# A hybrid block and two diffusion-transformer layers in float32 on one Trainium2 core: head-norm factors on 128 partitions, single-stream weights 64 bytes on, and four smaller edits

## The chip, the cores and the metric

One NeuronCore of a Trainium2 chip runs the whole program; seven cores are idle. The metric is the device time of one execution in microseconds (us). The kernel before was run three times: 2473.56, 2482.21 and 2483.57 us, median 2482.21.

## The reference, cut to what matters

All inputs and results are float32. A first block (attention in three dilations, a state-space scan, a gated feed-forward network) acts on 256 tokens `x` of width 1024. A second block of two layers acts on `x` and on 256 context tokens `xc`, each layer with its own modulation vectors.

```python
def first_block(x, ...):
    h = x + hybrid_mixer(rmsnorm(x, norm1_w), w_in, conv_w, ...)   # q,k,v,z,xbc,dt,gates = xn @ w_in
    h = h + swiglu(rmsnorm(h, norm2_w), w_ffn_in, w_ffn_out)       # D_FF = 2816
    return rmsnorm(h, final_norm_w)

def second_block(x, c, ctx, ...):
    xc = ctx
    for l in range(2):
        mx, mc = split(silu(c) @ w_mod[l] + b_mod[l], 9), split(silu(c_ctx) @ w_mod[l] + b_mod[l], 9)
        x  = x  + 0.5 * mx[2] * swiglu_2(modulate(rms_norm(x),  mx[0], mx[1]), *ffn1)
        xc = xc + 0.5 * mc[2] * swiglu_2(modulate(rms_norm(xc), mc[0], mc[1]), *ffn1)
        h, hc = modulate(rms_norm(x), mx[3], mx[4]), modulate(rms_norm(xc), mc[3], mc[4])
        if l == 0: y, y_c = mix_window_diff(h, hc, ab_w_in, ab_w_out, ...)          # windowed + differential attention
        else:      y, _   = mix_mla_neighbourhood(h, hc, cd_w_in, cd_w_out, ...)    # latent + neighbourhood attention
        x = x + mx[5] * y
        x = x + 0.5 * mx[8] * swiglu_2(modulate(rms_norm(x), mx[6], mx[7]), *ffn2)
        if l == 0: xc = ...  # the same with mc, y_c
    return x

def head_norm(t, gain):              # on every head of q and k in both mixers
    return t * rsqrt(mean(t * t, over the head's 64, 96 or 32 channels) + 1e-6) * gain
```

The causal convolution of the first block has 4 taps and a bias per channel (`conv_w`, `conv_b`). The neighbourhood attention adds a bias of 8 heads that depends on the row and column distance of query and key (`rpb`).

## The kernel before, in words

**Products.** Activations lie with channels on partitions and tokens along the free dimension. Every weight matrix is streamed once, 128 x 1024 floats (512 KB) at a time: SP issues the load (`load_raw`, L113, five buffers `wraw`), ACT rounds a copy to the short float format (`wh`, L120), DVE forms the remainder `wl = raw - wh` (L121); `wh` and `wl` have five buffers each in the pool `wsplit`. The activations are split in the same way (`ah`, `al`; hidden activations `hh`, `hl`). A product of one 128-channel block is three matmuls on PE, `mm3_k`: `wh` by `ah` (L139), `wh` by `al` (L140), `wl` by `ah` (L141), and eight (or six) such blocks add up in one PSUM tile `pm`. The weight tile is the stationary operand and the activation the moving one; in `v_units` (L1165 to L1167), which makes values with tokens on partitions, it is the other way round.

**Streams and units.** `run` goes through a list of units (one stationary tile, one PSUM tile) and of steps woven between them. In the second block, two streams "c" (context) and "x" go side by side: their activations interleave in the tiles `comb`, so that one matmul has 512 columns. The first three units of a run (`head`) and its last ones (`edge`, up to three tiles) are done for each stream alone, with 256 columns. Where a list runs for one stream (the first block, queries, the last network), all matmuls have 256 columns.

**Addresses.** Pools are laid one behind the other in each partition's memory, and unused tiles (`gap`) shift what follows. A weight tile of 1024 floats begins 64 bytes past a multiple of 128; so do the tiles `comb` (also for one stream of them) and the hidden activations of the two-stream networks. The activations of the first block's mixer, its hidden activations and the tile of the last single-stream network begin at a multiple of 128. The split queries `hq`, `lq` begin 96 past a multiple of 128. In what follows "phase" is an address's remainder by 128 bytes.

**Head norms** (`HeadNorm`, in both mixers). Per product block the squares of the heads are summed by a matmul (L1047), the factors `rs` are computed for all blocks of a group, transposed (L1056) and split into one ring tile `rh` of 48 rows: high parts on rows 0 to n-1, low parts on rows 32 to 32+n-1, zeros between. `finish` then spreads a head's factor over its channels with a matmul whose stationary operand is the constant `sel` (48 rows, ones where a factor belongs), L1071, and DVE multiplies by it. These steps are deferred by `later` and so land between the matmuls of other units.

**First block's start.** SP loads `cols` (all small per-channel constants). On DVE, `start` halves the convolution weights, `cw = 0.5 * cols[...]` (L908). The squares of `x` are summed by DVE into `acc` (L322), PE sums them over channels (L345), DVE and ACT take the root, PE spreads the factor (L353) and the first product can start. On POOL's queue the constants and the first block's attention bias (`brow`) are moved.

**Neighbourhood bias.** `bias_rows` copies the 8 heads' rows 64 times into a scratch tensor in DRAM with 8 transfers of POOL's queue (L1643), DRAM to DRAM. In `mix_cd`, `load_bias` fetches for each head four 64 x 256 pieces from it (L1614, SP's queue) and POOL adds a mask (L1615); four buffers `bias`. `scores_d` asks for the bias two heads ahead and DVE adds it to the scores (L1623). The scores' softmax tiles `e` are a ring of eight in each mixer.

**Differential attention** (`attend_b` in `mix_ab`): scores (L1339, `qbx` 512 columns), softmax, transposes (L1140), values (L1355) and, after four heads, `normed`: a norm over the head's 128 channels with a square tile `ybs` of its own.

**Order.** The scheduler orders every engine's list by the order of the program and by which buffers come free; `mod_tasks` gives 72 pieces per layer of the modulation product (a load `wraw<-w_mod` and one or two DVE operations, L1001) that are woven into the networks.

Of the kernel before, what the change touches and what calls it, by code (L numbers as in the profile page):

```python
# [8 lines left out]
F32 = mybir.dt.float32  # L9
F32R = mybir.dt.float32r  # L10
AF = mybir.ActivationFunctionType
ALU = mybir.AluOpType
# [4 lines left out]
T = 256  # L17
# [51 lines left out]
class Builder:  # L69
    def __init__(self, ctx, tc, A):  # L70
        self.tc, self.nc, self.A, self.ctx = tc, tc.nc, A, ctx
        nc = self.nc
# [3 lines left out]

        self.gap(self.pool(ctx, "gap", 1), 320)
        self.tp = self.pool(ctx, "tmp", 10)
# [36 lines left out]

    def split_w(self, raw, f):
        nc = self.nc
        h = self.w_p.tile([128, 1024], F32R, name="wh")
        lo = self.w_p.tile([128, 1024], F32R, name="wl")
        nc.scalar.copy(h[:, :f], raw[:, :f])  # L120
        nc.vector.tensor_tensor(lo[:, :f], raw[:, :f], h[:, :f].bitcast(F32), op=ALU.subtract)  # L121
        return h, lo
# [79 lines left out]
    def run(self, items, streams, done=None, ko=0, ahead=2):  # L202
# [7 lines left out]
        def prepare(i):  # L210
            if i >= len(units) or i in ready:
                return
            u = units[i]
            f = u.src.shape[2]
            ready[i] = [self.split_w(self.load_raw(u.src[j]), f) for j in range(u.at, u.at + u.n)]

# [247 lines left out]
def block1(K, start_mod):  # L464
# [442 lines left out]
    def start():  # L907
        nc.vector.tensor_scalar(cw, K.cols[:, at:at + 120], 0.5, None, op0=ALU.mult)  # L908

# [178 lines left out]
def head_selectors(K, pool, width, rows, n):  # L1088

    nc, A = K.nc, K.A  # L1090
    at, n2 = COLS[f"sum{width}"]
    sums = K.cols[:rows, at:at + n2]
    raw = K.raw_p.tile([128, 1024], F32, name="wraw")
    sel = pool.tile([48, n * 128], F32R, name=f"sel{width}")
    nc.scalar.dma_start(raw[:48, :n * 128], A[f"sel{width}"])
    nc.vector.tensor_copy(sel, raw[:48, :n * 128])
    return sums, sel


def stacked(K, pool):  # L1100

    zero = K.t1("zero")
    K.nc.vector.memset(zero, 0.0)
    ring = []
    for i in range(4):
        ring.append(pool.tile([48, T], F32R, name=f"rh{i}"))
        K.nc.scalar.copy(ring[i], zero[:48])
    return ring
# [72 lines left out]
def mix_ab(K, streams):  # L1181
# [192 lines left out]
    def normed(po):  # L1374
        yb = sp.tile([128, 4, 128], F32, name="yb", bufs=2)
        nc.scalar.copy(yb, po.rearrange("p (h e) -> p h e", h=4))
        sq = sp.tile([128, 4, 128], F32, name="ybs", bufs=1)
        ss = sp.tile([128, 4], F32, name="yss", bufs=2)
# [32 lines left out]
def mix_cd(K, streams):  # L1411
# [195 lines left out]
    def load_bias(hd):  # L1607
        bias = biases[hd] = sp.tile([128, 2, T], F32, name="bias", bufs=4)
        for t in range(2):
# [28 lines left out]

def bias_rows(K):

    K.rpb = K.dram.tile([64, 8, 7 * 127], F32, name="rpb")
    rows = K.A["rpb"][:, 4:11].rearrange("h r c -> h (r c)").unsqueeze(0).to_broadcast([8, 8, 7 * 127])
    return [lambda i=i: K.nc.gpsimd.dma_start(K.rpb[8 * i:8 * i + 8], rows) for i in range(8)]  # L1643


def block2(K, layers=(0, 1)):
    nc, A = K.nc, K.A
    for layer in layers:
        both = ["c", "x"]

        def norms(i, layer=layer):
            return lambda s: K.norm_stream(s, K.mod(layer, s, i + 1), K.mod(layer, s, i))

        steps = K.pieces(40)
        if layer == 0:
            steps[10:10] = bias_rows(K)
        fctx = ExitStack()
        hid_p = K.pool(fctx, "h1", 14)
        K.ffn(A[f"f1g{layer}"], A[f"f1u{layer}"], [A[f"f1d{layer}{i}"] for i in range(3)], both,
# [96 lines left out]
def constants():  # L1756
# [25 lines left out]
    for name, rows, n in (("sel64", [64, 64], 5), ("sel96", [64, 32], 4)):  # L1782
        sel = np.zeros((48, n, 128), f)
        for b in range(n):
            at = 0
            for e, r in enumerate(rows[:2]):
                sel[[2 * b + e, 32 + 2 * b + e], b, at:at + r] = 1.0
                at += r
        c[name] = sel.reshape(48, n * 128)
    t = np.arange(T)  # L1790
# [131 lines left out]
```

## Time and profile before

| what | value |
|---|---|
| three runs | 2473.56, 2482.21, 2483.57 us (median 2482.21) |
| the profiled execution's own time | 2473.19 us |
| its span, first to last instruction | 2471.4 us |
| mean granted TensorE clock | 0.985 |
| PE busy | 2415.3 us, 98% of the span |
| PEld (weight loads, beside PE) | 2101.6 us, 85% |
| DVE / ACT / POOL busy | 1642.8 / 1064.7 / 34.3 us |
| read from HBM | 359.33 MB, 147 GB/s over the span |

The profiled execution stands 9.0 us under the median of the three runs. Matmuls overlap one another in the trace: one of 256 columns lasts 0.28 us, but the next starts some 0.12 us after it, so rates are read from the distance of the starts, or from the count in a window.

### The profile page before, as it was taken

The numbers are of one execution on the slowest core, as the hardware profiler recorded it, in microseconds if no ns is written. First come the engines' busy times: TensorE is split into PE (matmuls) and PEld (weight loads), VectorE is DVE, ScalarE is ACT, GpSimd is POOL, SyncE is SP. The second block draws the span as 40 slices with busy tenths as digits, with TensorE's granted clock in tenths as the row PEclk, the third lists the DMA queues.
The fourth block names the chain that finished last, engine by engine and source line by source line (L and its number), as shares of the span: only waits on it lengthen the run. The fifth ranks groups of instructions, "written<-read, shape, count | busy, mean of one in ns | idle before, by whom it ended". The sixth has DMA issues, their size and how long they took to land.

```text
span 2471.4 us, 38395 instructions
## 1 busy us (share of the span) xinstructions
PE 2415.3 (98%) x15104; PEld 2101.6 (85%) x15104; DVE 1642.8 (66%) x3016; ACT 1064.7 (43%) x1934; POOL 34.3 (1%) x56
## 2 busy tenths in 40 slices
PE   7999999999999999999999999999999999999999
PEld 6998999999988888886498888888888888876999
DVE  5767787787865666778757666656555555667655
ACT  4566565535632222535743222243222234555443
POOL 3000000000000000000000000000000000000000
PEclk9999899999999999999899999999999999999999
DMA  9455455676454554341014555534555422233554
GB/s 271 153 154 157 134 175 174 212 251 225 148 177 136 170 173 144 112 139 52 1 52 154 165 159 162 165 108 142 180 166 171 150 87 84 100 97 86 169 195 133
DMA packets 113157, 363.38 MB, mean 147 GB/s; under 512 B 21186, under 2 KB 23562, under 8 KB 112976
## 3 DMA queue, kind: packets, MB, share of 16 engines
q1 hardware_dynamic: 109232, 352.58, 45.1%
q0 software_dynamic: 2176, 5.09, 0.9%
q10 hardware_dynamic: 1568, 3.25, 0.4%
q8 instruction: 119, 1.95, 0.3%
q14 instruction: 62, 0.51, 0.1%
HBM read 359.33 MB, written 3.36 MB: 147 GB/s over the span
## 4 chain that ended last, share of the span: by engine, by line
PE 70%; DVE 3%; ACT 2%; issue 1%; DMA 0%; ACTq 0%; DVEq 0%
PE pm L139 20%; PE pm L140 20%; PE pm L141 20%; PE pt L1140 1%; PE pa L1047 1%; PE pm L1339 1%; PE pt L1071 1%; PE pa L1592 1%; DVE wl L121 1%; PE pm L1600 1%; PE pa L1355 1%; PE pm L1279 1%; PE pa L1316 0%; PE pm L1622 0%; PE pm L1165 0%
## 5 line engine op out<-in xcount | busy, mean ns | idle before, releaser
L139 PE MATMUL pm<-ah,wh 128*128 128x256 f32 (+2 forms) x3096 | 1002.9, 326 | 13.1 <-ACT ah L370 10.7
L140 PE MATMUL pm<-al,wh 128*128 128x256 f32 (+2 forms) x3096 | 997.4, 323 | 1.1 <-DVE al L371 1.0
L141 PE MATMUL pm<-ah,wl 128*128 128x256 f32 (+2 forms) x3096 | 996.1, 322 | 0.0
L120 ACT CAST wh<-wraw 128x1024 fp32r<-128x1024 f32 (+4 forms) x535 | 541.0, 1014 | 946.0 <-PE pm L140 750.3
L121 DVE TENSOR_TENSOR wl<-wraw,wh 128x1024 fp32r<-128x1024 f32 (+4 forms) x535 | 627.5, 1176 | 228.3 <-ACT wh L120 225.8
L139 PEld LDWEIGHTS pm<-ah,wh 128*128 128x128 f32 (+1 forms) x3096 | 590.1, 192 | 67.8 <-ACT ah L370 12.3
L140 PEld LDWEIGHTS pm<-al,wh 128*128 128x128 f32 (+1 forms) x3096 | 591.9, 191 | 49.0 <-issue 2.7
L141 PEld LDWEIGHTS pm<-ah,wl 128*128 128x128 f32 (+1 forms) x3096 | 592.2, 191 | 46.6 <-issue 2.3
L140 PE MATMUL pm<-hl,wh 128*128 128x512 f32 (+1 forms) x934 | 312.6, 335 | 0.0
L139 PE MATMUL pm<-hh,wh 128*128 128x512 f32 (+1 forms) x934 | 312.1, 334 | 0.0
L141 PE MATMUL pm<-hh,wl 128*128 128x512 f32 (+1 forms) x934 | 312.1, 334 | 0.0
L1001 DVE SCALAR_TENSOR_TENSOR junk<-wraw,cactc 128x1024 f32<-128x1024 f32 x112 | 137.2, 1225 | 183.1 <-DMA wraw<-w_mod 183.0
L1001 DVE SCALAR_TENSOR_TENSOR junk<-wraw,cactx 128x1024 f32<-128x1024 f32 x144 | 176.1, 1223 | 48.8 <-DMA wraw<-w_mod 46.2
L139 PEld LDWEIGHTS pm<-hh,wh 128*128 128x128 f32 x934 | 175.7, 188 | 18.7
L140 PEld LDWEIGHTS pm<-hl,wh 128*128 128x128 f32 x934 | 175.7, 188 | 18.6
L141 PEld LDWEIGHTS pm<-hh,wl 128*128 128x128 f32 x934 | 175.8, 188 | 18.4
L125 ACT CAST hh<-g 128x512 fp32r<-128x512 f32 (+1 forms) x113 | 59.1, 525 | 228.4 <-DVE g L428 228.4
L428 DVE TENSOR_TENSOR g<-g,pm 128x512 f32<-128x512 f32 (+1 forms) x113 | 64.0, 567 | 55.6 <-PE pm L141 54.1
L126 DVE TENSOR_TENSOR hl<-g,hh 128x512 fp32r<-128x512 f32 (+1 forms) x113 | 63.9, 567 | 0.3
L458 DVE SCALAR_TENSOR_TENSOR xc<-pm,mcol0c,xc 128x256 f32<-128x256 f32 x56 | 26.9, 481 | 53.5 <-PE pm L141 53.3
L424 ACT ACTIVATE g<-pm 128x512 f32<-128x512 f32 (+1 forms) x116 | 55.9, 486 | 2.0 <-PE pm L141 2.0
L1140 PEld LDWEIGHTS pt<-ident,e 128*128 128x128 f32 x272 | 30.7, 145 | 22.0 <-issue 18.6
(425 smaller groups left out, 2260.0 us busy)
## 6 DMA issues: line engine op xcount, KB each, us to landing
wraw<-w_mod SPq DMA_DIRECT2D x144, 512.0 KB, 4.0
wraw<-f1g SPq DMA_DIRECT2D x44, 512.0 KB, 3.9
wraw<-f1u SPq DMA_DIRECT2D x44, 512.0 KB, 4.2
wraw<-f2g SPq DMA_DIRECT2D x44, 512.0 KB, 3.6
wraw<-f2u SPq DMA_DIRECT2D x44, 512.0 KB, 3.6
wraw<-f1d SPq DMA_DIRECT2D x32, 512.0 KB, 3.9
wraw<-f2d SPq DMA_DIRECT2D x32, 512.0 KB, 3.6
wraw<-w_xbc SPq DMA_DIRECT2D x24, 512.0 KB, 3.7
```

Of the source, the lines that this page charges most:

```text
L120: nc.scalar.copy(h[:, :f], raw[:, :f])
L121: nc.vector.tensor_tensor(lo[:, :f], raw[:, :f], h[:, :f].bitcast(F32), op=ALU.subtract)
L125: self.nc.scalar.copy(h, src)
L126: self.nc.vector.tensor_tensor(lo, src, h.bitcast(F32), op=ALU.subtract)
L139: nc.tensor.matmul(out, h[:, c], ah, start=first, stop=False)
L140: nc.tensor.matmul(out, h[:, c], al, start=False, stop=False)
L141: nc.tensor.matmul(out, lo[:, c], ah, start=False, stop=last)
L424: nc.scalar.activation(half(g["g"], s), p, AF.Silu)
L428: nc.vector.tensor_tensor(t, t, p, op=ALU.mult)
L458: self.nc.vector.scalar_tensor_tensor(x, p, gate, x, op0=ALU.mult, op1=ALU.add)
L1001: nc.vector.scalar_tensor_tensor(junk, raw, 1.0, K.cact[s], op0=ALU.mult, op1=ALU.mult, accum_out=K.mcol[layer, s][:, j:j + 1])
L1140: nc.tensor.transpose(p[:, j * 128:(j + 1) * 128], b, K.ident)
```

## The change

1. **Weight tiles.** `split_w` makes tiles of 1088 floats and uses 1024 of them, from float 16 on (64 bytes) where a unit is worked on for one stream alone and its activations come from `comb`, else from float 0. The gap in front of what follows falls from 320 to 64 bytes (the ten tiles grow by 2560 bytes together), so later tiles keep their phase.
2. **Head norms.** `sel` and the ring tiles `rh` have 128 rows; the added rows are zero.
3. **`start`** halves the convolution weights on GpSimd.
4. **`bias_rows`** loads the 8 heads' rows into a tile of 8 partitions and copies them from there, later; it is called once the first network's pool is open.
5. **`normed`** takes its square tile from the ring `e`.
6. **`load_bias`** has three buffers in place of four.

```diff
-        self.gap(self.pool(ctx, "gap", 1), 320)
+        self.gap(self.pool(ctx, "gap", 1), 64)
...
-    def split_w(self, raw, f):
+    def split_w(self, raw, f, at=0):
         nc = self.nc
-        h = self.w_p.tile([128, 1024], F32R, name="wh")
-        lo = self.w_p.tile([128, 1024], F32R, name="wl")
+        h, lo = (self.w_p.tile([128, 1088], F32R, name="w" + n)[:, at:at + 1024] for n in "hl")
...
-            ready[i] = [self.split_w(self.load_raw(u.src[j]), f) for j in range(u.at, u.at + u.n)]
+
+            if two:
+                alone = len(u.streams or streams) == 1 or i < head or i >= n - edge
+            else:
+                alone = self.comb and not self.single and u.lin and u.lin[0] == self.acts
+            ready[i] = [self.split_w(self.load_raw(u.src[j]), f, 16 if alone else 0) for j in range(u.at, u.at + u.n)]
...
     def start():
-        nc.vector.tensor_scalar(cw, K.cols[:, at:at + 120], 0.5, None, op0=ALU.mult)
+        nc.gpsimd.tensor_scalar(cw, K.cols[:, at:at + 120], 0.5, None, op0=ALU.mult)
...
-    sel = pool.tile([48, n * 128], F32R, name=f"sel{width}")
-    nc.scalar.dma_start(raw[:48, :n * 128], A[f"sel{width}"])
-    nc.vector.tensor_copy(sel, raw[:48, :n * 128])
+    sel = pool.tile([128, n * 128], F32R, name=f"sel{width}")
+    nc.scalar.dma_start(raw[:, :n * 128], A[f"sel{width}"])
+    nc.vector.tensor_copy(sel, raw[:, :n * 128])
...
-        ring.append(pool.tile([48, T], F32R, name=f"rh{i}"))
-        K.nc.scalar.copy(ring[i], zero[:48])
+        ring.append(pool.tile([128, T], F32R, name=f"rh{i}"))
+        K.nc.scalar.copy(ring[i], zero)
...
-        sq = sp.tile([128, 4, 128], F32, name="ybs", bufs=1)
+        sq = sp.tile([128, 512], F32, name="e", tag="e", bufs=8).rearrange("p (h e) -> p h e", h=4)
...
-        bias = biases[hd] = sp.tile([128, 2, T], F32, name="bias", bufs=4)
+        bias = biases[hd] = sp.tile([128, 2, T], F32, name="bias", bufs=3)
...
-def bias_rows(K):
+def bias_rows(K, pool):
 
     K.rpb = K.dram.tile([64, 8, 7 * 127], F32, name="rpb")
-    rows = K.A["rpb"][:, 4:11].rearrange("h r c -> h (r c)").unsqueeze(0).to_broadcast([8, 8, 7 * 127])
-    return [lambda i=i: K.nc.gpsimd.dma_start(K.rpb[8 * i:8 * i + 8], rows) for i in range(8)]
+    rows = pool.tile([8, 896], F32, name="rpbrow", bufs=1)[:, :7 * 127]
+    copies = rows.unsqueeze(1).to_broadcast([8, 8, 7 * 127])
+    steps = [lambda: K.nc.gpsimd.dma_start(rows, K.A["rpb"][:, 4:11].rearrange("h r c -> h (r c)"))]
+    return steps + [lambda i=i: K.nc.gpsimd.dma_start(K.rpb[8 * i:8 * i + 8].rearrange("q h u -> h q u"), copies)
+                    for i in range(8)]
...
-        if layer == 0:
-            steps[10:10] = bias_rows(K)
-        fctx = ExitStack()
-        hid_p = K.pool(fctx, "h1", 14)
+        if layer == 0:
+            steps[10:10] = bias_rows(K, hid_p)
...
-        sel = np.zeros((48, n, 128), f)
+        sel = np.zeros((128, n, 128), f)
...
-        c[name] = sel.reshape(48, n * 128)
+        c[name] = sel.reshape(128, n * 128)
```

Three of the edits move instructions. First, POOL's queue from the program's start, before (`mk` are attention masks, `bt` the one-hot table, `rpb` the neighbourhood bias, `brow` and `bias` the first block's own):

```order
L519 DMA mk_136<-mask 128x128
L519 DMA mk_138<-mask 128x128
L1643 DMA rpb<-rpb 64x1x889
L508 DMA brow_108<-ct 8x16x384
L508 DMA brow_109<-ct 8x16x256
```

and with the change:

```order
L523 DMA mk_136<-mask 128x128
L523 DMA mk_138<-mask 128x128
L912 ISA
L912 TENSOR_SCALAR cw<-cols 128x120
L512 DMA brow_108<-ct 8x16x384
L512 DMA brow_109<-ct 8x16x256
```

The halving `cw`, which was the first DVE operation after the memsets (in front of the sums `acc` of L322), stands on POOL between the masks and `brow`; the copy `rpb` has left this place.

Second, SP's queue around the neighbourhood attention (`dmask` is its mask, `f2g` and `f2u` the next network's weights), before:

```order
L113 DMA wraw<-cd_out 128x1024 x8
L1604 DMA dmask<-dmask 128x256
L1614 DMA bias<-rpb 64x4x64 x16
L113 DMA wraw<-f2g 128x1024
L113 DMA wraw<-f2u 128x1024
L1614 DMA bias<-rpb 64x4x64 x16
L113 DMA wraw<-f2g 128x1024
```

and with the change:

```order
L113 DMA wraw<-cd_out 128x1024 x8
L1608 DMA dmask<-dmask 128x256
L1618 DMA bias<-rpb 64x4x64 x12
L113 DMA wraw<-f2g 128x1024
L113 DMA wraw<-f2u 128x1024
L1618 DMA bias<-rpb 64x4x64 x20
L113 DMA wraw<-f2g 128x1024
```

Four bias loads, those of the fourth head, have moved from the first group to the second.

Third, PE's list in the differential attention's second half (`kb`, `qbx` keys and queries, `e` softmax tiles, `pts` their transposes, `yb` the normed outputs), before:

```order
L1339 MATMUL pm<-kb,qbx 128x512
L1355 MATMUL pa<-v,pts 128x128 x2
L1339 MATMUL pm<-kb,qbx 128x512 x5
L1364 MATMUL pt<-ident,yb 128x128 x4
L1140 MATMUL pt<-ident,e 128x128 x2
L1339 MATMUL pm<-kb,qbx 128x512
L1355 MATMUL pa<-v,pts 128x128 x2
L1140 MATMUL pt<-ident,e 128x128 x8
```

and with the change:

```order
L1343 MATMUL pm<-kb,qbx 128x512 x3
L1144 MATMUL pt<-ident,e 128x128 x2
L1343 MATMUL pm<-kb,qbx 128x512
L1144 MATMUL pt<-ident,e 128x128 x2
L1359 MATMUL pa<-v,pts 128x128 x4
L1368 MATMUL pt<-ident,yb 128x128 x4
L1144 MATMUL pt<-ident,e 128x128 x2
L1343 MATMUL pm<-kb,qbx 128x512 x2
```

The run of five score matmuls has broken into smaller groups between transposes.

## Rows read from the trace of the kernel before

**Rows 1.** The page: busy time by engine, and the last chain's shares by engine.

```profile
PE 2415.3 (98%) x15104; PEld 2101.6 (85%) x15104; DVE 1642.8 (66%) x3016; ACT 1064.7 (43%) x1934; POOL 34.3 (1%) x56
...
PE 70%; DVE 3%; ACT 2%; issue 1%; DMA 0%; ACTq 0%; DVEq 0%
```

**Rows 2.** Windows of PE: start:end, us, busy (matmuls), granted clock, DMA share, GB/s.

```profile
484.00:510.00 26.00, 26.00 (x219) 1.00 0.77 257
512.00:532.00 20.00, 20.00 (x178) 1.00 0.69 227
540.00:575.00 35.00, 34.98 (x291) 1.00 0.77 262
2300.00:2335.00 35.00, 35.00 (x311) 1.00 0.67 224
700.00:740.00 40.00, 40.00 (x178) 1.00 0.51 157
```

**Rows 3.** Timeline of PE, latent values: start, us, engine, line, operation, tiles.

```profile
2153.91 0.28 PE L1524 MATMUL pm<-wl,hk 128*128 128x256 f32 x1
...
2154.98 0.28 PE L1524 MATMUL pm<-wl,hk 128*128 128x256 f32 x1
```

**Rows 4.** Windows of all engines (PE, PEld, DVE, ACT, POOL), first block's network.

```profile
540.00:580.00 40.00, 39.98 (x333) 39.69 (x332) 35.44 (x56) 19.99 (x32) 0.00 (x0) 1.00 0.79 267
```

**Rows 5.** Timeline there: DVE's remainder and its first use.

```profile
562.81 1.22 DVE L121 TENSOR_TENSOR wl<-wraw,wh 128x1024 fp32r<-128x1024 f32 x1
...
564.76 0.28 PE L141 MATMUL pm<-ah,wl 128*128 128x256 f32 x1
```

**Rows 6.** Instructions of L1071: count, min/median/max ns, first and last start.

```profile
L1071 PE MATMUL pt<-rh,sel x64: 276/356/384, 1077.4 to 2187.3; 48*128 48x256 f32 x38, 48*64 48x256 f32 x16, 48*96 48x256 f32 x10
```

**Rows 7.** Timeline of PE, values with L1071 between them.

```profile
1135.18 0.38 PE L1071 MATMUL pt<-rh,sel 48*128 48x256 f32 x1
...
1135.74 0.30 PE L1165 MATMUL pa<-wh,ah 128*128 128x320 f32 x1
1135.98 0.38 PE L1071 MATMUL pt<-rh,sel 48*128 48x256 f32 x1
...
1137.34 0.31 PE L1166 MATMUL pa<-wh,al 128*128 128x320 f32 x1
1137.49 0.31 PE L1167 MATMUL pa<-wl,ah 128*128 128x320 f32 x1
```

**Rows 8.** Timeline of the weight loads there.

```profile
1135.60 0.19 PEld L1165 LDWEIGHTS pa<-wh,ah 128*128 128x128 f32 x1
1135.97 0.18 PEld L1071 LDWEIGHTS pt<-rh,sel 48*128 48x128 f32 x1 [0.19 <-issue]
```

**Rows 9.** Timeline of PE: a transposition on 128 rows, and 64-column selectors.

```profile
1098.07 0.60 PE L1056 MATMUL pt<-ident,rs 128*8 128x128 f32 x4
1098.42 0.48 PE L139 MATMUL pm<-ah,wh 128*128 128x512 f32 x1
...
2145.66 0.33 PE L1071 MATMUL pt<-rh,sel 48*64 48x256 f32 x1
...
2146.46 0.33 PE L1071 MATMUL pt<-rh,sel 48*64 48x256 f32 x1
```

**Rows 10.** Timeline of DVE and PE at the start.

```profile
9.19 0.22 DVE L908 TENSOR_SCALAR cw<-cols 128x120 f32<-128x120 f32 x1 [7.78 <-DMA cols<-cols]
...
15.59 1.02 PE L345 MATMUL pt<-ones,acc 128*128 128x1 f32 x4 [3.78 <-DVE acc L322]
```

**Rows 11.** Timeline of SP, DVE and POOL, neighbourhood attention.

```profile
2224.82 12.33 SPq L1614 DMA_DIRECT2D bias<-rpb  x16
...
2229.41 1.27 POOL L1615 TENSOR_TENSOR bias<-bias,dmask 128x512 f32<-128x512 f32 x1 [27.20 <-DMA bias<-rpb]
...
2230.38 0.43 DVE L1623 TENSOR_TENSOR pm<-pm,bias 128x256 f32<-128x256 f32 x1 [0.42 <-PE pm L1622]
```

**Rows 12.** Windows of PE, differential attention (columns as in rows 2).

```profile
1216.00:1230.00 14.00, 13.68 (x38) 0.51 0.00 0
```

More of the change, by code (lines that the diff above doesn't have):

```diff
@@ L1652, in norms @@
             return lambda s: K.norm_stream(s, K.mod(layer, s, i + 1), K.mod(layer, s, i))
+        fctx = ExitStack()
+        hid_p = K.pool(fctx, "h1", 14)
         steps = K.pieces(40)
         if layer == 0:
-            steps[10:10] = bias_rows(K)
-        fctx = ExitStack()
-        hid_p = K.pool(fctx, "h1", 14)
+            steps[10:10] = bias_rows(K, hid_p)
         K.ffn(A[f"f1g{layer}"], A[f"f1u{layer}"], [A[f"f1d{layer}{i}"] for i in range(3)], both,
```

## The prediction

> **What bounds the kernel now.** The page's busy times come first: PE is busy for 98% of the span, and 70% of the last chain runs over it [rows 1]. So time goes only where PE's matmuls follow one another faster, or where PE stood still. The reader should see next that "busy" hides two rates. In the windows [rows 2], all at full clock, 256-column matmuls start every 26.0/219 = 0.1187 us and 35/291 = 0.1203 us where weight tile and activation have the same phase (484 to 510, 540 to 575), but every 20/178 = 0.1124 and 35/311 = 0.1125 us where they are 64 bytes apart (512 to 532, the down products; 2300 to 2335, the last network). The timelines give 0.120 and 0.1133 when no count is cut off at a window's edge; I use 0.0066 us as the difference. Third, the head norms: L1071 is 64 matmuls on 48 rows [rows 6] set between matmuls on 128.
>
> **Weight tiles 64 bytes on.** This changes no instruction, only addresses. From the code, the matmuls whose two operands go from the same phase to 64 apart are 44 x 24 = 1,056 in the first block's network and 1,908 elsewhere: heads of three two-stream networks 432, their tails 324, `ab_qk` 144, `ab_out` 288, `cd_ckv` 96, `cd_cq` 144, `cd_dq` 96, and 384 in the two value products, where weight and activation trade roles. The 144 of the split queries stay 32 bytes apart as before; nothing is counted for them. No row shows a weight at phase 0 beside an activation at 64, the new pair. The nearest is the latent value product, its stationary operand at 96 and its moving one at 64: nine starts from 2153.91 to 2154.98 are 0.119 apart [rows 3], between the two rates. So the distance seems to count, not which of the two is shifted. Bounds: 0 and 0.0066 us each; I take 0.0066, because the pairs 64 bytes apart all show it.
>
> In the first block's network it would be 1,056 x 0.0066 = 7.0 us. But there 16 pieces of the modulation product share DVE and the transfers: DVE is busy 35.4 of 40 us and the transfers 0.79 at 267 GB/s [rows 4], and a remainder that ends at 562.81 + 1.22 = 564.03 is used at 564.76 [rows 5]. PE can gain only those 0.7 us of slack up to about 570 us, some 0.5 in the down products before, and 1.6 in the last ten units: 2.8 us. Elsewhere 1,908 x 0.0066 = 12.6 us, less 5 x 72 x 0.0066 = 2.4 us in five places where the context stream's head precedes a wait for the norm of "x" (a faster head only waits longer). **Sum: 2.8 + 10.2 = 13.0 us**, bounds 0 and 19.6.
>
> A rule speaks against this part. The Trainium skill, "TensorE: Matmul & The Clock Gate", section "Step-by-step: what each phase is for", says that PE reads weights and moving operand through two independent ports, so that loading the next weights takes nothing from the running matmul. By it the term would be zero; the two rates at one clock [rows 2] disagree with it.
>
> **Selectors on 128 rows.** Between L1071 at 1135.18 and the next at 1135.98 lie two value matmuls; these follow each other in 0.15 us when undisturbed (1137.34, 1137.49) [rows 7]. So one L1071 takes 0.80 - 2 x 0.15 = 0.50 us, against 0.12 for 256 columns in a dense flow: 0.38 too much. The load rows say where: an ordinary load begins 0.14 us before its matmul (1135.60 for 1135.74), that of `sel` with its matmul (1135.97 for 1135.98) after 0.19 us of idleness [rows 7, 8]. What an insertion of full rows costs is shown by the transpositions: two from 1098.07 to 1098.42 take 0.35 us for 4 x 128 columns, 0.225 at the dense rate of 40/178 us per 512 columns [rows 2, 9], so 0.06 each too much. I let 0.09 stay and take 0.29 for each isolated selector of 128 columns: 23 x 0.29 = 6.7 us. Seven pairs, with one change each, 7 x 0.26 = 1.8. Fifteen of 64 columns: from 2145.66 to 2146.46, 0.80 us hold three matmuls of 0.12 and one selector of 0.44 [rows 9], 0.32 too much, of which 0.23 may go: 3.5. Five of 96 columns 1.3, the other seven 1.8. That is 15.1 us. I take off 1 us, as a 64-column load may still not be drawn ahead, and another 1.6 us, a tenth, for places where a faster PE would meet the weights' supply; both are my choice. **12.5 us**, bounds 0 and 16. The larger `sel` transfer and ring copies have as many elements per partition as before and come long before use.
>
> By another rule of the Trainium skill ("TensorE: Matmul & The Clock Gate", section "The mechanism"), a weight load overlaps a running matmul only where the row groups differ; after the change all are alike, and the term would be zero. Against it, loads of full rows start 0.14 us ahead of their matmuls here [rows 8].
>
> **Start.** DVE waited 7.78 us for `cols` and then ran `cw` [rows 10], with the sums `acc` queued behind. On POOL, `cw` stands before `brow`, which waits for later data anyway. The chain `acc`, L345 at 15.59, root, L353, first product can begin one or two sums earlier, but DVE's row copies stay in its list: **0.7 us** gained, bounds 0 and 1.2; if POOL's operation is late, the first block's convolution, which comes after the first queries and keys, still covers it.
>
> **Bias loads.** With three buffers, head 3 waits for head 0's last addition, and so stands where head 4 stood: first issue 2224.82, mask operation 2229.41, ready 2230.68; the addition ran at 2230.38 [rows 11]. That is 0.3 us late, and heads 5 and 7 come within 0.3 us of their use by the same interval of 5.86 us from release to ready. **1.0 us** lost, bounds 0 and 4 (all five later heads late by 0.8). Behind them on SP stand the last network's weights, four loads (12.33/16 x 4 = 3.1 us) later; the whole output product `cd_out` covers it.
>
> **The rest.** The copies of the bias rows move into the second block's first network and are wanted only in its last mixer: nothing. The square tile in the ring `e` reorders PE, DVE and ACT in the differential attention. The clock there falls to the lower level, 1.2 GHz, for most of 14 us [rows 12]. I take 0; bounds -5 (half the stretch back) and +6 (as much again).
>
> **Sum:** 13.0 + 12.5 + 0.7 - 1.0 = 25.2 us less. On the profiled execution, 2473.2, this gives 2448.0; that execution is 9.0 us below the median of the runs, 2482.2, from which the forecast is **2457.0 us**.
>
> **Rivals.** (a) *Weight phase gains nothing*: a weight at 0 beside an activation at 64 runs at 0.120, since the activation's own phase is what counts. For it: in every fast row the activation is at 0; against: rows 3. Then 12.2 us less: 2470.0; chance 0.11. The Trainium skill's rule of the two ports ends at the same time. (b) *The selectors gain nothing*: the delay comes from the break in the flow (another PSUM tile, another address), not from rows. For it: after the wider selectors a delay remains with 64 columns too; against: the transpositions break the flow as much [rows 9]. 12.7 us less: 2469.5; chance 0.09. The Trainium skill's rule on row groups ends there too. (c) *Neither does what it says*: the rest alone, 2482.5; chance 0.05. (d) *Slower*: the pitch of the weight tiles grows from 4096 to 4352 bytes, so that successive tiles alternate between two places in 512 bytes. The 4,762 matmuls of 512 columns keep their phase by 128, but if they are sensitive to 512 they pay. Their 0.2247 us [rows 2] are 0.0114 above 512 columns at 2.4 GHz, so there is room for better as for worse. At 0.0066 us each the price is 31.4 us: 6.2 us net, 2488.4; from 5.3 ns the gain is gone, and from 7.9 ns it is slower by more than 0.5%. Nothing in the trace of before speaks for it; chance 0.05.
>
> **How the numbers follow.** The forecast has 0.70. About 0.5% (12.4 us: 2469.8 to 2494.6) is what a measurement of this kernel can tell from no change. Rivals (a) and (b) fall on that edge and are halved. Faster by more: 0.70 + 0.10 = 0.80; within: 0.10 + 0.05 + 0.02 = 0.17; slower by more: 0.03. The forecast's own range is 2446 (both terms near their upper bounds) to 2467 (13 us lost in unknown costs); to hold 8 in 10 it must reach to the edge of (a) and (b), and a few us of scatter between runs are added below: 2443 to 2472.
>
> **What would show it.** Right: the windows of the first block's network show 0.113 us per matmul after 580 us, and in 540 to 575 waits for `wl` or `wraw` in place of the gain; in the head and tail units 0.113; L1071 with loads ahead of their matmuls and 0.2 us or less between neighbours; windows of 512 columns still at 0.2247. Wrong: 0.120 with new addresses (a), 0.3 us around 128-row selectors (b), or 512-column matmuls slower (d); a longer low-clock stretch in the differential attention, or additions L1623 that wait for POOL by more than 1 us in sum, would each take a few us back.

## The result, and the profile after

The changed kernel takes 2452.26 us (median of 4 runs, 2446.17 to 2458.18) against 2478.95 us before (median of 4, 2473.56 to 2483.57): ratio 0.9888, 95% interval 0.9857 to 0.992, or 26.7 us less. The forecast was 25.2 us less, with 2443 to 2472 as its range. The sum was right; its terms were not, as the stages show.

The page of the changed kernel, the rows that answer to [rows 1] (lines behind the edits have moved by one to four: L138 to L140 are L139 to L141 of before, L1075 is L1071):

```profile
PE 2388.2 (97%) x15104; PEld 2089.9 (85%) x15104; DVE 1641.4 (67%) x3015; ACT 1066.4 (44%) x1936; POOL 35.5 (1%) x58
...
PE 68%; DVE 3%; ACT 2%; DMA 1%; issue 1%; ACTq 0%; DVEq 0%; SPq 0%
```

PE is still what bounds the kernel; its busy time fell by 27.1 us. Its windows, as [rows 2], with one of the differential attention at the end:

```profile
484.00:510.00 26.00, 26.00 (x232) 1.00 0.74 251
512.00:532.00 20.00, 19.42 (x164) 1.00 0.73 236
540.00:575.00 35.00, 33.43 (x282) 1.00 0.75 251
2300.00:2335.00 35.00, 35.00 (x311) 1.00 0.66 195
700.00:740.00 40.00, 39.97 (x177) 1.00 0.66 208
1205.00:1235.00 30.00, 26.05 (x126) 1.00 0.00 1
```

The first window went from 219 to 232 matmuls: by this count 0.1121 us each, as forecast. But the next two hold fewer than before, 164 for 178 and 282 for 291, and PE is no longer busy throughout. So what the first block's network gained up to 510 us it gave back behind, in this execution. The 512-column window is as before. In the last one the clock is at its higher level throughout, where it stood at the lower for 14 us [rows 12].

The head norms, L1075 by instruction and in PE's timeline among the value matmuls, with the weight loads there:

```profile
L1075 PEld LDWEIGHTS pt<-rh,sel x64: 132/186/193, 1083.6 to 2166.0; 128*128 128x128 f32 x38, 128*64 128x64 f32 x16, 128*96 128x96 f32 x10
L1075 PE MATMUL pt<-rh,sel x64: 277/283/387, 1083.7 to 2166.1; 128*128 128x256 f32 x38, 128*64 128x256 f32 x16, 128*96 128x256 f32 x10
```

```profile
1136.13 0.31 PE L1171 MATMUL pa<-wl,ah 128*128 128x320 f32 x1
1136.28 0.29 PE L1075 MATMUL pt<-rh,sel 128*128 128x256 f32 x1
1136.42 0.31 PE L1169 MATMUL pa<-wh,ah 128*128 128x320 f32 x1
1136.56 0.30 PE L1170 MATMUL pa<-wh,al 128*128 128x320 f32 x1
1136.70 0.28 PE L1075 MATMUL pt<-rh,sel 128*128 128x256 f32 x1
1136.82 0.31 PE L1171 MATMUL pa<-wl,ah 128*128 128x320 f32 x1
```

```profile
1136.19 0.19 PEld L1075 LDWEIGHTS pt<-rh,sel 128*128 128x128 f32 x1
...
1136.57 0.19 PEld L1075 LDWEIGHTS pt<-rh,sel 128*128 128x128 f32 x1
```

Two value matmuls and one selector now take 1136.70 - 1136.28 = 0.42 us, not 0.80 [rows 7]. The selector's load begins 0.09 and 0.13 us ahead of its matmul, not with it [rows 8], and the next matmul follows it in 0.12 to 0.14 us, the dense rate: nearly all of the 0.38 us is gone, not 0.29 of it.

At the start the halving is on POOL, and the chain [rows 10] begins earlier:

```profile
9.30 0.51 POOL L912 TENSOR_SCALAR cw<-cols 128x120 f32<-128x120 f32 x1 [5.20 <-DMA cols<-cols]
...
15.02 1.02 PE L349 MATMUL pt<-ones,acc 128*128 128x1 f32 x4 [3.78 <-DVE acc L326]
```

L349 starts at 15.02 instead of 15.59, 0.57 us earlier.

What the forecast had at nothing is the bias copies. The instructions of L1649 (8 transfers out of 8 partitions), the windows behind them, and the modulation product that waited there:

```profile
L1649 POOL DMA_DIRECT2D rpb<-rpbrow x8: 562/562/607, 654.5 to 658.4; - x8
...
DMA to landing us min/median/max: 10.9/22.1/32.8
```

```profile
650.00:680.00 30.00, 28.13 (x198) 1.00 0.95 99
680.00:700.00 20.00, 17.97 (x73) 0.91 0.77 158
```

```profile
693.11 1.23 DVE L1005 SCALAR_TENSOR_TENSOR junk<-wraw,cactc 128x1024 f32<-128x1024 f32 x1 [17.12 <-DMA wraw<-w_mod]
```

The transfers land up to 32.8 us after their issue. For 30 us the DMA engines are busy for 0.95 of the time and move only 99 GB/s; the modulation weights come late, DVE, which does their products in order, waits 17.12 us for one of them, and PE waits for DVE's gate product `g` (L432) behind it:

```profile
PE pm L138 <- DVE g L432: 2.0, 1, 2.0
```

So PE issues 73 matmuls in a window that held 90 at the dense rate; its clock falls to the lower level in part of it (0.91 granted). In the kernel before, the same eight copies, from DRAM and in the program's first 60 us (L1643), landed much sooner:

```profile
DMA to landing us min/median/max: 7.8/9.0/10.6
```

### Where the time went, stage by stage

The distance in us of two matmuls that can be found in each trace by weight and number; the columns are single executions of the kernel before, the changed kernel, and experiments e1, e9, e10 and e11 below.

| stage | before | after | e1 | e9 | e10 | e11 |
|---|---|---|---|---|---|---|
| first block's mixer, 231 to 297 us | 65.68 | 65.49 | 54.45 | 61.88 | 59.26 | 65.52 |
| SSM output product | 46.09 | 47.58 | 47.58 | 47.56 | 46.09 | 46.09 |
| first block's network | 190.97 | 192.60 | 190.91 | 191.68 | 190.85 | 189.61 |
| two-stream network, 684 to 714 us | 29.92 | 33.81 | 29.92 | 29.92 | 29.92 | 33.91 |
| its rest, with 108 tail matmuls | 299.78 | 299.85 | 299.79 | 299.79 | 299.54 | 299.52 |
| queries and keys, second half | 66.35 | 64.39 | 64.41 | 64.39 | 64.39 | 64.39 |
| `ab_v`, values | 38.71 | 34.23 | 34.23 | 34.23 | 34.23 | 34.24 |
| differential attention | 94.13 | 88.71 | 89.95 | 91.10 | 88.73 | 88.72 |
| `ab_out` | 53.72 | 51.90 | 53.73 | 52.75 | 51.84 | 51.87 |
| latent queries to last `cd_dv` | 84.65 | 73.27 | 73.81 | 73.82 | 73.16 | 73.26 |
| latent and neighbourhood attention | 51.67 | 51.94 | 51.89 | 52.19 | 51.53 | 51.81 |
| last network | 171.13 | 171.13 | 171.13 | 171.13 | 171.13 | 177.84 |

Most stages repeat within 0.1 us in kernels that have the same edits there. Those that don't are the ones that teach something: the mixer of the first block, whose half-clock stretch near 240 us comes and goes in kernels that don't differ there; the SSM output product and the last network, which take either of two times; and the first block's network, which takes 192.60 and 189.61 us in two executions of one program (after, e11).

### The profile page after: what moved, and what is told of

Its sections match the earlier page's. It is cut to its first block, busy times and chain, and to the rows that moved or that the text cites. A ratio compares the mean times of both kernels' runs of the same rounds, so it can differ in the third digit from the quotient of the medians.

```text
span 2450.1 us, 38416 instructions
## 1 busy us (share of the span) xinstructions
PE 2388.2 (97%) x15104; PEld 2089.9 (85%) x15104; DVE 1641.4 (67%) x3015; ACT 1066.4 (44%) x1936; POOL 35.5 (1%) x58
## 4 chain that ended last, share of the span: by engine, by line
PE 68%; DVE 3%; ACT 2%; DMA 1%; issue 1%; ACTq 0%; DVEq 0%; SPq 0%
PE pm L138 20%; PE pm L139 20%; PE pm L140 20%; PE pt L1144 1%; DMA wraw<-w_mod 1%; PE pa L1051 1%; PE pa L1596 1%; DVE wl L120 1%; PE pm L1283 1%; PE pm L1626 0%; PE pa L1320 0%; PE pm L1604 0%; DVE al L375 0%; ACT wh L119 0%; ACT e L1124 0%
## 5 line engine op out<-in xcount | busy, mean ns | idle before, releaser
L138 PE MATMUL pm<-ah,wh 128*128 128x256 f32 (+2 forms) x3096 | 999.8, 325 | 16.6 <-ACT ah L374 10.7
L139 PE MATMUL pm<-al,wh 128*128 128x256 f32 (+2 forms) x3096 | 993.4, 322 | 0.8 <-DVE al L375 0.7
L140 PE MATMUL pm<-ah,wl 128*128 128x256 f32 (+2 forms) x3096 | 993.1, 322 | 0.0
L138 PEld LDWEIGHTS pm<-ah,wh 128*128 128x128 f32 (+1 forms) x3096 | 588.3, 191 | 71.6 <-ACT ah L374 12.4
L139 PEld LDWEIGHTS pm<-al,wh 128*128 128x128 f32 (+1 forms) x3096 | 589.6, 191 | 48.1 <-issue 2.7
L140 PEld LDWEIGHTS pm<-ah,wl 128*128 128x128 f32 (+1 forms) x3096 | 589.3, 190 | 46.8 <-issue 2.3
L139 PE MATMUL pm<-hl,wh 128*128 128x512 f32 (+1 forms) x934 | 313.4, 336 | 0.2 <-DVE hl L125 0.2
L138 PE MATMUL pm<-hh,wh 128*128 128x512 f32 (+1 forms) x934 | 312.8, 335 | 0.6 <-DVE xx L462 0.6
L140 PE MATMUL pm<-hh,wl 128*128 128x512 f32 (+1 forms) x934 | 312.8, 335 | 0.0
L138 PEld LDWEIGHTS pm<-hh,wh 128*128 128x128 f32 x934 | 175.8, 188 | 19.3 <-issue 0.8
L139 PEld LDWEIGHTS pm<-hl,wh 128*128 128x128 f32 x934 | 175.9, 188 | 18.9 <-DVE hl L125 0.4
L140 PEld LDWEIGHTS pm<-hh,wl 128*128 128x128 f32 x934 | 175.4, 188 | 18.6
L432 DVE TENSOR_TENSOR g<-g,pm 128x512 f32<-128x512 f32 (+1 forms) x113 | 63.9, 565 | 51.4 <-PE pm L140 50.0
L1144 PEld LDWEIGHTS pt<-ident,e 128*128 128x128 f32 x272 | 29.2, 141 | 25.9 <-issue 18.9
```

Of the source, the lines that this page charges most:

```text
L138: nc.tensor.matmul(out, h[:, c], ah, start=first, stop=False)
L139: nc.tensor.matmul(out, h[:, c], al, start=False, stop=False)
L140: nc.tensor.matmul(out, lo[:, c], ah, start=False, stop=last)
L432: nc.vector.tensor_tensor(t, t, p, op=ALU.mult)
L1144: nc.tensor.transpose(p[:, j * 128:(j + 1) * 128], b, K.ident)
```

## The experiments

**e1, the selectors alone.**

```diff
-    sel = pool.tile([48, n * 128], F32R, name=f"sel{width}")
+    sel = pool.tile([128, n * 128], F32R, name=f"sel{width}")
...
-        ring.append(pool.tile([48, T], F32R, name=f"rh{i}"))
+        ring.append(pool.tile([128, T], F32R, name=f"rh{i}"))
```

> The kernel before with the 128-row selectors and ring tiles alone. If the ledger of the two traces is read rightly, the selectors are worth more than forecast: the two head-norm stretches (window before 1077 to 1145 and 2102 to 2187) become 3 to 5 and 10 to 12 us shorter, the span 14 to 18 us shorter than 2471.4. The forecast's own term was 12.5 us. Rival (b), that the break in the flow costs and not the row count: 0 to 2 us.

Measured: 2452.15 us (5 runs), ratio 0.9903 (0.987 to 0.9935): 25.7 us less than the kernel before in the same series (2477.8), nearly the whole gain of the change. By the stages, though, the selectors are worth less: queries and keys 1.9, values 4.5, latent part 10.8, and 0.3 in two small stages not shown: 17.5 us. Its span (2440.8) is shorter by 30.6 us, since stretches of half clock fell out as well, worth 11.2 us in the mixer of the first block, where nothing was changed, and 4.2 in the differential attention; some 2.3 us were lost elsewhere, 1.5 of them in the SSM output. Rival (b), the break in the flow, falls: e1 breaks it in the same places.

**e2, 64 rows.**

```diff
-    sel = pool.tile([48, n * 128], F32R, name=f"sel{width}")
+    sel = pool.tile([64, n * 128], F32R, name=f"sel{width}")
...
-        ring.append(pool.tile([48, T], F32R, name=f"rh{i}"))
+        ring.append(pool.tile([64, T], F32R, name=f"rh{i}"))
```

> As e1, but with 64 rows instead of 128. If what costs is a weight load for a part of the array's rows, 64 rows cost as much as 48: L1071 still shows 0.3 us to both neighbours, the gain is 0 to 2 us. If it is the odd number 48, or the break in the flow, 64 rows do as well as 128 (14 to 18 us, or 0 to 2 us in e1 also).

Measured: 2476.90 us (one run); the three head-norm stages are 66.35, 38.72 and 84.65 us, those of the kernel before. L1071 there, with the durations of [rows 6]:

```profile
L1071 PE MATMUL pt<-rh,sel x64: 276/356/384, 1080.4 to 2190.9; 64*128 64x256 f32 x38, 64*64 64x256 f32 x16, 64*96 64x256 f32 x10
```

And its loads among the value matmuls:

```profile
1138.24 0.18 PEld L1071 LDWEIGHTS pt<-rh,sel 64*128 64x128 f32 x1 [0.19 <-issue]
1138.24 0.38 PE L1071 MATMUL pt<-rh,sel 64*128 64x256 f32 x1
1138.55 0.19 PEld L1167 LDWEIGHTS pa<-wl,ah 128*128 128x128 f32 x1
1138.55 0.41 PE L1167 MATMUL pa<-wl,ah 128*128 128x320 f32 x1
```

The load of 64 rows starts with its matmul, and so does the load of all rows behind it: neither is ahead. So what costs is an operand on a part of the array's rows between operands on all, not the odd 48; 48 and 64 rows are the two sizes tried. For columns it is otherwise: the selectors of 64 and 96 columns got their gain in e1 and in the change.

**e3, the square tile in the ring alone.**

```diff
-        sq = sp.tile([128, 4, 128], F32, name="ybs", bufs=1)
+        sq = sp.tile([128, 512], F32, name="e", tag="e", bufs=8).rearrange("p (h e) -> p h e", h=4)
```

> The kernel before with only the square tile in the ring e. Theory: the differential attention's new order gives the 8.8 us by which the stretch from the value product to the output product shrank, less what the selectors gave in it: 4 to 7 us shorter between the last value product and the first output product, nothing elsewhere. Rival: the reordering gives nothing (my forecast of 0), and that stretch shrank because it began at another clock: within 1 us.

Measured: 2468.53 us (one run). The attention stage takes 89.81 us (94.13 before) and `ab_out` 52.75 (53.72). The window of [rows 12], now in e3:

```profile
1216.00:1230.00 14.00, 12.66 (x66) 1.00 0.00 0
```

The stretch at half clock that lasted 13.7 us from 1216 [rows 12] is gone; in its place 6.8 and 3.4 us of half clock stand earlier, from 1133, and cost 2.9 us in the values (41.61 for 38.71). With the selectors as well, seven of the eight profiled executions have no such stretch (88.7 us) and one, e9, has 6.8 us of it (91.10). So most of the 5.4 us are time at the lower clock. Which edit brings them is not shown: the ring alone (e3) takes 4.3 us off this stage, but moves 2.9 us of loss into the values; the selectors alone (e1, without the ring) take 4.2 us off it and have 6.8 us at half clock there; e9, with both, has as much. "Nothing elsewhere" did not hold either: `ab_out` is 1.0 us shorter in e3.

**e5, the moved weights alone** (with e3's ring and three bias buffers, whose memory they need).

```diff
-        h = self.w_p.tile([128, 1024], F32R, name="wh")
-        lo = self.w_p.tile([128, 1024], F32R, name="wl")
+        h, lo = (self.w_p.tile([128, 1088], F32R, name="w" + n)[:, at:at + 1024] for n in "hl")
...
```

With the ring but four bias buffers (e4) the larger tiles do not fit into the memory of a partition (a pool of 31.19 KB meets 29.25 KB), so there is no time for it.

> The kernel before with the moved weight tiles; the square tile in the ring e and three bias buffers come with them, since the larger weight tiles need their memory (e3 showed the ring alone: no half-clock stretch near 1216). Outside the differential attention, the forecast is 13.0 us less. Theory from the trace after: matmuls 64 bytes apart have two rhythms, 0.113 and 0.118 us, and the new pitch lets whole units fall into the second, the SSM output product and the first block's down products among them (0.113 before). Single-stream units of the second block then gain 0.002 to 0.003 us per matmul, 3 to 5 us in all, and the first block loses 1 to 3 us. The clock stretch at 240 us may be there or not and is left out by comparing stage by stage.

Measured: 2467.54 us (10 runs, 2453.34 to 2479.22), ratio 0.9984 (0.9954 to 1.0013): no difference that can be told, where the forecast's 13.0 us would have shown. Matmuls of 256 columns whose weights moved start 0.115 to 0.118 us apart in the mean, 0.120 before. But the last network, whose phases the change doesn't touch, took 177.85 us instead of 171.13, all its matmuls at 0.118. The pitch theory was half right: there are two rhythms.

**e7, one pitch**, in the changed kernel.

```diff
-        h, lo = (self.w_p.tile([128, 1088], F32R, name="w" + n)[:, at:at + 1024] for n in "hl")
+        w = self.w_p.tile([128, 2176], F32R, name="w")
+        h, lo = w[:, at:at + 1024], w[:, at + 1024:at + 2048]
```

> The changed kernel with each weight's two parts in one tile of 8704 bytes (17 x 512), so that all tiles of both parts have the same place in 512 bytes (in the change the pitch of 4352 makes them alternate). Theory: the rhythm goes with the distance of weight and activation by 512 bytes: 64 gives 0.113 always, 320 gives either. Here 64: first block's mixer except the SSM output, all single-stream units of the second block, the first block's up products; these show 0.113 everywhere. 320: SSM output, down products, last network: some of them at 0.118 (the last network is at 0.113 in both kernels). Rival: the rhythm falls at random after a stall, whatever the address: no unit group changes to 0.113 throughout.

Measured: 2455.23 us (one run). With a distance of 64 by 512 bytes the up products of the first block ran at 0.118 (median); with 320 the last network ran at 0.113. That is against the theory by address; the rival, a rhythm that is found at run time, stands. e11 below shows two rhythms of one program, without any edit.

**e8, the 512-column units moved too**, in e7's kernel.

```diff
+            alone = alone or two
             ready[i] = [self.split_w(self.load_raw(u.src[j]), f, 16 if alone else 0) for j in range(u.at, u.at + u.n)]
```

> As e7, and the 512-column units of the second block are moved by 64 bytes too, so that weight and activation are 64 bytes apart there as well (same phase before). If a same-phase pair costs a fixed 0.0066 us per matmul whatever the columns, 4,764 matmuls go from 0.2267 to 0.220 us: 31 us less. If the wider matmul hides it, they stay at 0.2267 and the time is that of e7.

Measured: 2484.38 us (one run), 29.2 us more than e7. A window of 512 columns, full clock:

```profile
720.00:760.00 40.00, 39.98 (x172) 1.00 0.56 184
```

172 matmuls in 40 us for 178 [rows 2]: by this count 0.233 us for 0.225, by the distance of the starts 0.233 to 0.235 for 0.2267. With 512 columns it is the same phase that is fast and 64 bytes apart that is slow, by 6 to 8 ns each over 4,764 matmuls. Neither of the two expectations had that sign.

**e6 and e10, the bias rows as before**, in the changed kernel; e10 repeats e6 beside e9 and e11.

```diff
...
-            steps[10:10] = bias_rows(K, hid_p)
+            steps[10:10] = bias_rows(K)
```

> The changed kernel with the bias rows copied as before (8 transfers from DRAM to DRAM, early). Theory: in the changed kernel the 8 copies out of 8 partitions hold the DMA engines at 0.95 for 30 us and starve the first network's weights; without them the 3.9 us lost between 684 and 704 us come back, and the half-clock stretch at 695 is gone: 4 us shorter there. Rival: the loss there came from the modulation pieces moved by one place; then it stays. My forecast took the copies as free.

> e6 again, on the same chip as e9 and with more rounds: differs from e9 only by the moved weights and the third bias buffer. Theory: within 4 us of e9 on either side. Forecast: 12 us faster than e9.

Measured: e6 2449.39 us (4 runs), ratio 0.9895 (0.986 to 0.9929), e10 2445.99 us (4 runs, 2442.21 to 2449.1), ratio of e10 0.9887 (0.9874 to 0.99). The stage from 684 us is back at 29.92 us. Windows of e10 where the copies stood:

```profile
650.00:680.00 30.00, 28.36 (x163) 0.94 0.38 120
680.00:700.00 20.00, 20.00 (x90) 1.00 0.60 201
```

The DMA share is 0.38 instead of 0.95 and the second window is dense again. The copies cost 3.9 us. The edit also takes back the one step that the load of the rows adds, so it does not by itself exclude the rival of the shifted modulation pieces; DVE's wait of 17.12 us for a transfer speaks against it. And it changes the copies' source and their time together: which of the two makes them slow is not separated.

**e9, the weights not moved**: the kernel before with e1's and e3's edits and this one, so that against e10 the moved weights and the third bias buffer are missing.

```diff
-        nc.vector.tensor_scalar(cw, K.cols[:, at:at + 120], 0.5, None, op0=ALU.mult)
+        nc.gpsimd.tensor_scalar(cw, K.cols[:, at:at + 120], 0.5, None, op0=ALU.mult)
```

> The kernel before with the 128-row selectors, the square tile in the ring and the convolution weights on GpSimd: no moved weight tiles, bias rows and four bias buffers as before. Theory: against the changed kernel it keeps the gains (selectors 14, no half-clock stretch near 1216 us 6, start 0.6), gets back 4 us at the bias copies and loses what the moved weights are worth, which is 0 to 4 us by the rhythm that the units fall into: 2445 to 2452 us, not slower than the changed kernel. By the forecast's 13 us for the moved weights it would be 9 us slower than the changed kernel.

Measured: 2455.77 us (6 runs), ratio 0.9924 (0.9904 to 0.9944), 9.8 us more than e10 by the medians. Both theories missed by the medians: e9 was to take 2445 to 2452 us and to be no slower than the changed kernel (2453.34 in e11), and e10 was to lie within 4 us of it; the forecast's 12 us is nearer. The stages that the moved weights touch differ by less: `ab_out` 0.9, latent part 0.7, the tail 0.25 (two more like it), 0.8 in the first block's network, some 0.8 in heads: 3 to 4 us. The rest of the two profiled executions' difference lies in half-clock stretches (3.4 us at 52 us, 6.8 at 1213 in e9 alone) and in the rhythm of the SSM output (47.56 and 46.09). How much these make over all runs can be estimated from the mean granted clock of each run. In the kernel before, 23.9 us at half clock cost 11.2 us in the first block's mixer against e1, which has none; over the span they lower the mean clock by 0.0048, so 0.001 of it is worth some 2.3 us. The mean times of e9 and e10 are 9.3 us apart, their mean clocks 0.9867 and 0.9888: by this estimate 4.8 us are clock, and 4.4 are left, near the 3 to 4 of the stages. In the same way e1 keeps some 20 of the 26 us between its mean and that of the kernel before, and e5, at the same clock as the kernel before, keeps its 3. Whether e9's lower clock comes from its edits or from chance isn't settled.

**e11, the changed kernel again**, without an edit.

> The changed kernel itself on the same chip: 3 to 5 us slower than e10 (the bias copies), if the copies are what costs; equal if not.

Measured: 2453.34 us (6 runs, 2440.79 to 2456.53), ratio 0.9906 (0.9888 to 0.9925), 7.4 us more than e10 by the medians, where 3 to 5 were expected; 4.0 of it is the copies' stage in the profiled executions. The same program as the one profiled first now shows other rhythms. Two windows of the first execution, and then of e11, all at full clock:

```profile
400.00:420.00 20.00, 20.00 (x172) 1.00 0.68 212
...
2300.00:2335.00 35.00, 35.00 (x311) 1.00 0.66 195
```

```profile
2300.00:2335.00 35.00, 35.00 (x299) 1.00 0.59 182
400.00:420.00 20.00, 20.00 (x179) 1.00 0.74 226
```

In the SSM output (400 to 420) e11 is the faster one, 179 for 172; in the last network the slower, 299 for 311. PE is busy throughout in all four. In the last network alone the choice is worth 6.7 us.

**e12, the first block's network alone with its weights.**

```diff
-            raw = K.load_raw(K.A[f"w_mod{layer}"][j])
-            for s in who:
+            skip = layer == 0 and j < 16
...
+            raw = None if skip else K.load_raw(K.A[f"w_mod{layer}"][j])
+            for s in () if skip else who:
```

> e6's kernel with the first 16 modulation pieces left out (no load, no product; their sums are set to zero), which in the other kernels run during the first block's network. If the weights' supply is what kept that network from becoming faster with moved weights (190.97 us in the kernel before, 190.84, 190.85 with the change and early bias rows), it now takes 186 to 188 us: 1,056 up and gate matmuls at 0.113 to 0.116 in place of 0.120, 528 down matmuls at 0.113 to 0.118 in place of 0.113. If supply was not the reason, it stays at 190 to 191 us.

Measured: the first block's network takes 187.11 us (one run). Windows of e12, and then one of the changed kernel:

```profile
533.00:570.00 37.00, 37.00 (x317) 1.00 0.62 185
560.00:600.00 40.00, 40.00 (x347) 1.00 0.62 189
```

```profile
533.00:570.00 37.00, 35.47 (x300) 1.00 0.76 262
```

The changed kernel has 300 matmuls in 533 to 570, and PE is busy for 35.47 us of them; here 317, busy throughout. So the modulation pieces are what took gain there. They are both loads and DVE's work on them, and e12 takes away both. In the changed kernel, from 500 to 580 us, PE waits for DVE, not for a weight, while DVE waits for the modulation weights:

```profile
PE pm L138 <- DVE g L432: 1.6, 3, 0.7
DVE junk L1005 <- DMA wraw<-w_mod: 11.0, 11, 1.8
```

## Why the prediction was right in sum and wrong in its terms

| term | forecast | measured by stages |
|---|---|---|
| moved weights | 13.0 less (2.8 in the first block's network) | 3 to 4 less (in the first block's network between 1.4 less and 1.6 more); 4.4 less as estimated from the runs of e9 and e10 |
| selectors | 12.5 less (15.1 before deductions) | 17.5 less |
| start | 0.7 less | 0.6 less |
| bias buffers | 1.0 more | 0.3 more or nothing |
| bias copies | 0 | 3.9 more |
| square tile, order, clock | 0 (bounds -5, +6) | 5.4 less in the attention (4.2 of it with the selectors alone), 1.0 in `ab_out` |

That the sum came out is luck. The forecast had some 9 us too much for the weights and 3.9 for the copies, and 5.0 too little for the selectors and some 6 for time at the lower clock, which it had at nothing. The medians are 26.7 us apart, the spans of the two profiled executions 21.3.

- **Moved weights: the step "I take 0.0066, because the pairs 64 bytes apart all show it" failed.** They don't all show it: such pairs run at 0.113 or at 0.118, and which one differs between groups of units in one execution and between executions of one program (e11). Same-phase pairs run at 0.120 in every kernel here that has them. A moved matmul gained 7 ns where it fell into the faster rhythm and 2 ns in the slower. The windows of [rows 2] at 0.1124 and 0.1125 were two that had the faster one, and they were taken for a constant, though the same trace has the other: its first block's mixer, with operands 64 bytes apart by the addresses given for it, in two windows of 14 us (columns as in rows 2), the SSM output product and then the output product `w_out`, whose starts are 0.113 and 0.118 us apart:

```profile
410.00:424.00 14.00, 14.00 (x126) 1.00 0.65 197
432.00:446.00 14.00, 14.00 (x121) 1.00 0.70 233
```

- **Moved weights in the first block's network.** That the modulation pieces take most of the gain there was right (e12). But the changed kernel loses more than that. By the distances of the starts in the two traces, the up products gained 4.7 us (0.1199 to 0.1153 us), the longer gaps (stalls, and matmuls at half clock at the network's start) grew by 4.1 us, and the down products, which the edit does not move, lost 2.3 us, as they ran at 0.118 here and at 0.113 in the kernel before: 1.6 us more in all. And the sign that was named, waits for `wl` or `wraw`, did not show: PE waits for `g`.
- **Selectors: right in place and cause, mis-sized by 5.0 us.** The 0.09 us that I let stay and both deductions (1 us for 64 columns, 1.6 for supply) were not there; the undeducted excess, 0.38 us for the isolated ones, was nearly all of it.
- **Bias copies: the step "wanted only in its last mixer: nothing" failed.** It asked who waits for the result, not what the transfers hold up. Out of 8 partitions they took the DMA engines for 30 us, in a stage in which DVE's products wait for the modulation weights.
- **Square tile: the value failed, and the bound was passed.** The bound of -5 was priced by the half-clock stretch, and that stretch went; with `ab_out` it is 6.4 us. That the square tile alone did it is not shown.
- **Bias buffers.** DVE's waits for POOL there are 1.5 us in two cases, for 0.4 in one, as the sum had it, but the stage, at 51.5 to 51.9 us with three buffers and 51.7 to 52.2 with four, is no longer: the waits do not show in PE's time.
- **Start:** as forecast.
- **Rivals.** (b) is excluded by e1, and e2 shows that the number of rows is what counts. (d), slower 512-column matmuls through the pitch, did not happen: their starts are 0.2267 us apart with either pitch. (a) lies nearer to the truth in its time than the forecast's own term, but not in its reason: the moved pairs do not stay at 0.120.

The runs agree with neither rule of the Trainium skill that the prediction names ("TensorE: Matmul & The Clock Gate"). The section "Step-by-step: what each phase is for" has weights and moving operand read through independent ports; moving one of them by 64 bytes changed the rate of a dense stream in both directions (0.120 to 0.113 or 0.118 us with 256 columns, 0.2267 to 0.233 or 0.235 with 512). The section "The mechanism" lists weight loads as overlapping with running matmuls only where row groups differ. Here full-row loads start 0.09 to 0.14 us ahead of their matmuls, beside full-row matmuls, and a 64-row load between them (e2) does not. The same section also lets a load be drawn ahead into a background weight buffer, which could be what the full-row loads do; no run here shows that buffer.

## What to carry to other kernels

A narrow operand padded with zeros to all 128 rows can be faster than the narrow one, where it stands between full matmuls: 64 of them gave 17.5 us. A transfer that nobody waits for still has a price, which is read from the DMA share of the stage that it lands in. And a rate that two windows of one execution share need not be a constant of the program: before a term is built on a difference of 6%, the rate has to be seen in every group of matmuls of its kind, and in a second execution. A good sum can hide four wrong terms.

## What the runs showed that was not expected

- PE has two steady rhythms for 256 columns and 64 bytes between the operands' phases, 0.113 and 0.118 us. In the last network one of them is kept throughout; in the first block's network of kernels with moved weights they change between groups of units. Two executions of one program differ (after, e11). What chooses is not settled: it is neither the address by 512 bytes (e7) nor the pitch (e1 and e9 have 0.118 in the SSM output with the old pitch). The down products of the first block's network are at 0.113 in all five kernels with unmoved weights.
- With 512 columns the preference turns round: 0.2267 us at the same phase, 0.233 to 0.235 at 64 bytes apart (e8).
- The half-clock stretch near 240 us lasts 24 us in the kernel before and in the changed one, 10 in e6 and e10, and is absent in e1, though e1 edits nothing there; it explains up to 11 us between profiled executions, more than most edits studied here.
- The version with the bias rows as before (e10) is the fastest by the medians: 2445.99 us beside 2453.34 for the changed kernel on the same chip; the intervals of their ratios overlap, but the copies' stage is 4 us shorter in each trace of it.
